# The first column tiles of a decoder step on x·g instead of the normalised x, with the factors applied at the end, and the sample states on column groups

## The chip, the cores and the metric

One core of a Trainium2 chip runs the whole program. The metric is the device time of one execution in microseconds (us). The engines are TensorE (PE: matmuls, and PEld: its weight loads), VectorE (DVE), ScalarE (ACT), GpSimd (POOL) and the queue of SyncE (SP), which here only issues DMAs.

## The reference, cut to what matters

One layer of a hybrid decoder for 1024 prompt tokens and 8 sample tokens (1032 columns in all), D = 1024, followed by a final norm:

```
h = rmsnorm(x, norm_g)               # x * rsqrt(mean(x^2) + eps) * g, per token
proj = h @ w_in                      # 7688 columns: q, k, v, beta, alpha, gate, u, v, ...
A) q, k, v = silu(causal_conv(...)); gated delta rule in chunks, one state per head
   sample tokens: S = a S + k (beta (v - a S^T k))^T ;  o = S^T q      (8 states x 4 heads)
B) chunked spatial gating:  u * (W_s layernorm(v) + b) * silu(gate)
C) cross-attention, 4 heads, into 256 memory tokens
merged = sum of sigmoid(gates) * (branch @ w_br);  y = rmsnorm(x + merged @ w_out)
```

Since a token's rsqrt factor is one number per token, (x·g·r) @ w equals ((x·g) @ w)·r.

## The kernel before, in words

Activations lie transposed: 128 channels on the partitions, 8 blocks k of channels, 1032 token columns. Every product is made of three passes of TensorE in a reduced format (fp32r): each operand is split in a rounded part `hi` and a rest `lo`, and `mm3` (L298) runs hi·hi, lo·hi and hi·lo, 24 matmuls for one group. `hTh` and `hTl` hold hi and lo of the normalised x for all columns. A column tile of `w_in` (128 output columns) is loaded (`w_load`), split by ACT and then DVE or POOL (`w_split`, L270), and multiplied with three groups of 344 token columns (`project`, L311). Two tiles are split ahead (`whi`, `wlo`, two buffers), four are loaded ahead (`raw`).

The order of all instructions is written out by hand. Long side chains are Python generators on a list `run`; `mm3` calls `tick()` after every sixth matmul, and each tick lets every generator emit its next piece, so the side work is strewn between the matmuls. Each engine runs its own instructions in the order in which they were emitted.

The opening (L361 to L550) cuts the columns in four parts (256, 256, 256, 264). For each part: `n_square` (L400) sums the squares of the untransposed x on ACT, `n_newton` (L404) takes the reciprocal root on DVE in 11 small instructions, `spread` (L317) makes a diagonal matrix of the factors on DVE and multiplies it with ones on PE, so that each partition has the token's factor, `scale` (L328, eight instructions) multiplies the transposed x by g and that factor in place, and `n_split` (L410) makes `hTh` and `hTl`. Then three column tiles ("k 0", "v 0", "bv 0") multiply that part, and ACT copies the results out (`evac`, L525; L534). Parts 1 to 3 are prepared by `norm_gen` while the matmuls of the part before run. Tile "q 0" follows as an ordinary `project` (L550), and then the narrow tile of 16 columns for beta and alpha (`wab2`, L580 to L588, 48 matmuls, "the ab stage" below), on which the gates and so the whole delta chain wait. The convolutions of k and v run on DVE (L500 to L507), that of q on POOL.

`sample_gen(h)` (L658) handles the 8 sample states of one head. Its matmuls (L687) take each state (128x128) as the weights and two columns (normalised k and q) as the moving operand: out comes S^T k and S^T q, with the channel on the partitions.

Of the kernel before, what the change touches and what calls it, by code (L numbers as in the profile page):

```python
# [151 lines left out]
def tile_mixer_step(ctx: ExitStack, tc: tile.TileContext, a):  # L152
# [175 lines left out]
    def scale(x, r, col, k):  # L328
        V.scalar_tensor_tensor(
            out=x[:, k], in0=x[:, k], scalar=colv[:, col + k:col + k + 1], in1=r, op0=ALU.mult, op1=ALU.mult  # L330
        )
# [68 lines left out]
    def n_square(i):  # L400
        x = xin[i][:rows[i]]
        S.activation(out=x, in_=x, func=AF.Square, accum_out=nss[:rows[i], i:i + 1])  # L402

    def n_newton(n):  # L404
        sl = slice(in_part[n][0], in_part[n][-1] + 1)
        x = nss[:, sl]
        V.tensor_scalar(out=x, in0=x, scalar1=1.0 / D, scalar2=EPS, op0=ALU.mult, op1=ALU.add)
        yield from rsqrt_ops(nrs[:, sl], x, f"n{n}")

    def n_split(n, b, eng=V):  # L410
        ks = slice(b * 4, b * 4 + 4)
        x, hi, lo = xT[n][:, ks], hTh[:, ks, part[n]], hTl[:, ks, part[n]]
        S.copy(out=hi, in_=x)
        eng.tensor_tensor(out=lo, in0=x, in1=f32(hi), op=ALU.subtract)

    def n_part(n):
        x = xT[n]
        r = spread(np_, nrs, [(i, rows[i]) for i in in_part[n]])
        yield
        for k in range(KT):  # L420
            scale(x, r, 0, k)
            if k % 2:
                yield
        n_split(n, 0)
        n_split(n, 1)
        done.add(("norm", n))

    n_square(0)
    n_square(1)
    for _ in n_newton(0):  # L430
        pass
    wsp = [w_split(0, eng=G), w_split(1, eng=G)]
    next(wsp[0])
    for _ in n_part(0):
        pass
    next(wsp[0], None)
    next(wsp[1])
    n_square(2)
    n_square(3)
    next(wsp[1], None)  # L440
    for _ in w_split(2, slow=False, eng=G, pool=np_):
        pass
    xt_load(2)
    x_load(5, 6)
    xt_load(3)
    x_load(7, 8)
    w_load(3)
    SP.dma_start(out=wab, in_=a["w_ab"])
    SP.dma_start(out=scT, in_=a["conv_old"])
    SP.dma_start(out=a["conv_kept"], in_=a["state_conv"][:, 1:3, :])  # L450

    def norm_gen():
        for n in range(1, 4):
            yield
            for i, _ in enumerate(n_newton(n)):
                if i % 4 == 3:
                    yield
            yield from n_part(n)
            if n < 3:
                for i in in_part[n + 1]:  # L460
                    n_square(i)
        split(wab2[:, :, 0:8], wab2[:, :, 8:16], wab)

    run.add(norm_gen())
# [48 lines left out]
    def qkv_tile(name, h):  # L513
        if name == "k":
            kq_t[h] = xp.tile([P, 2, NT], F32, tag="kq", name="kq")
            v_t[h] = xp.tile([P, NT], F32, tag="vt", name="vt")
# [5 lines left out]
        raw = xp.tile([P, 3 + NT], F32, tag="xraw", name="xraw", bufs=2)
        G.memset(raw[:, 0:3], 0.0)

        def evac(n, sl, o):  # L525
            S.copy(out=raw[:, 3 + sl.start:3 + sl.stop], in_=o)  # L526
# [10 lines left out]
    w3 = [splits.pop(i) for i in range(3)]
    for n in range(4):
        run.until(lambda: ("norm", n) in done)
        for i, (w, ev) in enumerate(zip(w3, evacs)):  # L540
            ev(NS - 1 if n == 3 else 0, *h_group(w, n, part[n]))
            if n == 3 and i == 0:
                w_load(4)
            if n == 3 and i == 1:
                for _ in w_split(3, slow=False):
                    pass
# [108 lines left out]

    ag_t = {}

    def sample_gen(h):  # L658
# [26 lines left out]
        r = tp()[:, 0:16].rearrange("p (b t) -> p t b", t=2)  # L685
        for b in range(NB):
            PE.matmul(r[:, :, b], lhsT=st[:, b], rhs=kqn[:, :, b], start=True, stop=True)  # L687
# [827 lines left out]
```

## Time and profile before

| what | value |
| --- | --- |
| median of 3 runs (lowest to highest) | 1172.46 us (1171.12 to 1173.76) |
| the profiled execution's own time | 1172.25 us |
| its span, first to last instruction | 1170.4 us |
| mean granted TensorE clock | 0.983 |
| PE busy | 1121.8 us (96%) |
| DVE busy | 614.2 us (52%) |
| ACT busy | 402.0 us (34%) |
| POOL busy | 231.3 us (20%) |

Busy times of an engine are sums of its instructions; what counts for the end is which engine is waited for in each stage. The profile gives, for every group of instructions, the idle time just before it and what ended it.

### The profile page before, as it was taken

The page shows a single profiled execution, that of the slowest core. Times are in us where ns is not written, and L with a number is a line of the kernel's source. Part 1 is how long each engine was busy: PE and PEld are TensorE (multiplying, and loading weights), DVE is VectorE, ACT ScalarE, POOL GpSimd, SP SyncE. Part 2 cuts the span into 40 slices and gives each one's busy share as a digit, 9 for nine tenths or more (in the row PEclk, how much of TensorE's full clock was granted, in tenths as well). Part 3 has the DMA queues.
Part 4 walks back from the last instruction along what each step waited for, and adds up shares of the span by engine and source line. Part 5 has one row for each costly group of instructions (what it writes and reads, how often), then busy time and mean ns, then how long its engine had stood idle before and what let it go on. Part 6 is the DMA issues. An engine that isn't in the chain of part 4 may idle for free.

```text
span 1170.4 us, 18943 instructions
## 1 busy us (share of the span) xinstructions
PE 1121.8 (96%) x7474; PEld 1072.8 (92%) x7474; DVE 614.2 (52%) x1534; ACT 402.0 (34%) x854; POOL 231.3 (20%) x394
## 2 busy tenths in 40 slices
PE   4699999999999999999899999899999999999997
PEld 4698999999999999999899999889999999998884
DVE  5553673477247635622376532646536256786554
ACT  3424323243333233323344313545445321232232
POOL 2015285035503550430033100101101000000000
PEclk8799999999999999999899999999999999999999
DMA  9022421232123312431544445344343356663221
GB/s 369 3 74 37 132 76 43 94 113 83 37 93 96 84 35 93 122 113 71 195 151 135 154 163 184 111 140 127 109 127 91 125 193 184 214 208 103 78 92 56
DMA packets 83034, 137.75 MB, mean 118 GB/s; under 512 B 21744, under 2 KB 51664, under 8 KB 82296
## 3 DMA queue, kind: packets, MB, share of 16 engines
q1 hardware_dynamic: 68960, 94.04, 24.6%
q10 hardware_dynamic: 13984, 42.49, 12.0%
q8 instruction: 59, 0.97, 0.3%
q14 instruction: 31, 0.25, 0.1%
HBM read 104.97 MB, written 31.64 MB: 117 GB/s over the span
## 4 chain that ended last, share of the span: by engine, by line
PE 86%; DVE 6%; ACT 3%; DMA 2%; issue 1%; SPq 0%; POOL 0%; ACTq 0%; DVEq 0%
PE pj L301 52%; PE dl L301 20%; PE dl L224 1%; PE tp L224 1%; PE dl L785 1%; ACT x L402 1%; PE dl L1133 1%; DVE wlo L279 1%; PE dl L919 1%; PE dl L895 1%; PE tp L1085 1%; PE dl L910 1%; PE dl L903 1%; PE tp L687 1%; DMA gcb<-gcd 1%
## 5 line engine op out<-in xcount | busy, mean ns | idle before, releaser
L301 PE MATMUL pj<-hTh,whi 128*128 128x344 f32 (+2 forms) x1464 | 284.6, 329 | 8.2 <-DVE ql L188 4.2
L301 PE MATMUL pj<-hTh,wlo 128*128 128x344 f32 (+2 forms) x1464 | 277.7, 324 | 0.0
L301 PE MATMUL pj<-hTl,whi 128*128 128x344 f32 (+2 forms) x1464 | 273.0, 325 | 0.0
L301 PEld LDWEIGHTS pj<-hTh,whi 128*128 128x128 f32 x1464 | 236.0, 193 | 11.3 <-DVE ql L188 4.5
L301 PEld LDWEIGHTS pj<-hTl,whi 128*128 128x128 f32 x1464 | 239.3, 193 | 0.9 <-issue 0.4
L301 PEld LDWEIGHTS pj<-hTh,wlo 128*128 128x128 f32 x1464 | 236.4, 191 | 1.5 <-issue 0.8
L279 DVE TENSOR_TENSOR wlo<-raw,whi 128x1024 fp32r<-128x1024 f32 (+1 forms) x89 | 97.5, 1095 | 45.4 <-ACT whi L276 45.2
L276 ACT CAST whi<-raw 128x1024 fp32r<-128x1024 f32 (+1 forms) x92 | 86.2, 937 | 75.7 <-PE dl L301 62.1
L839 POOL TENSOR_TENSOR itmp<-X,Lt 128x60 f32<-128x60 f32 (+24 forms) x124 | 53.0, 428 | 171.8 <-DMA Lt<-ld 162.5
L958 ACT COPY stg<-pj 128x344 f32<-128x344 f32 x72 | 32.1, 446 | 126.2 <-PE pj L301 122.5
L1190 POOL TENSOR_TENSOR kvt<-kvt,qb 128x1024 f32<-128x1024 f32 x8 | 19.3, 2433 | 215.0 <-DMA kvt<-cache_mem_v 215.0
L301 PE MATMUL dl<-yh,whi 128*128 128x344 f32 x288 | 57.4, 321 | 0.0
L301 PE MATMUL dl<-yl,whi 128*128 128x344 f32 x288 | 57.1, 320 | 0.0
L301 PE MATMUL dl<-yh,wlo 128*128 128x344 f32 x288 | 57.1, 320 | 0.0
L845 POOL TENSOR_TENSOR X<-X,itmp 128x60 f32<-128x60 f32 (+24 forms) x124 | 47.1, 380 | 9.7
L301 PEld LDWEIGHTS dl<-yl,whi 128*128 128x128 f32 x288 | 47.8, 188 | 0.0
L301 PEld LDWEIGHTS dl<-yh,whi 128*128 128x128 f32 x288 | 47.7, 188 | 0.0
L301 PEld LDWEIGHTS dl<-yh,wlo 128*128 128x128 f32 x288 | 47.5, 188 | 0.0
L526 ACT COPY xraw<-pj 128x344 f32<-128x344 f32 (+2 forms) x38 | 16.3, 430 | 89.0 <-PE pj L301 88.9
L907 DVE COPY y<-dl 128x128 f32<-128x128 f32 x32 | 9.3, 292 | 61.2 <-PE dl L905 39.9
L1373 DVE TENSOR_TENSOR stg<-dl,stg 128x344 f32<-128x344 f32 x48 | 24.7, 514 | 18.0 <-PE dl L301 18.0
L498 POOL TENSOR_TENSOR kq<-kq,cvt 128x512 f32<-128x512 f32 x24 | 33.5, 1394 | 1.9
(371 smaller groups left out, 1569.5 us busy)
## 6 DMA issues: line engine op xcount, KB each, us to landing
raw<-w_tiles ACTq DMA_DIRECT2D x65, 512.0 KB
gate<-stg SPq DMA_DIRECT2D x23, 516.0 KB
stg<-gate SPq DMA_DIRECT2D x23, 516.0 KB
raw<-w_br ACTq DMA_DIRECT2D x24, 256.0 KB
x<-x_prompt SPq DMA_DIRECT2D x8, 512.0 KB
kvt<-cache_mem_k SPq DMA_DIRECT2D x16, 256.0 KB
kvt<-cache_mem_v SPq DMA_DIRECT2D x16, 256.0 KB
wor<-w_out SPq DMA_DIRECT2D x8, 512.0 KB
```

The costliest lines, as they stand in the source:

```text
L224: PE.transpose(out, in_, ident[:p, :p])
L276: S.copy(out=hi, in_=raws[i])
L279: eng.tensor_tensor(out=lo, in0=raws[i], in1=f32(hi), op=ALU.subtract)
L301: PE.matmul(out, lhsT=w, rhs=r, start=(i == 0), stop=(i == len(ops) - 1))
L402: S.activation(out=x, in_=x, func=AF.Square, accum_out=nss[:rows[i], i:i + 1])
L498: G.tensor_tensor(out=d[:, cs], in0=d[:, cs], in1=o, op=ALU.add)
L526: S.copy(out=raw[:, 3 + sl.start:3 + sl.stop], in_=o)
L839: G.tensor_tensor(out=tm, in0=X[:, 0:m, j:j + 1].to_broadcast([P, m, n]), in1=Lt[:, j:j + 1, j + 1:32].to_broadcast([P, m, n]), op=ALU.mult,)
L845: G.tensor_tensor(out=X[:, 0:m, j + 1:32], in0=X[:, 0:m, j + 1:32], in1=tm, op=ALU.subtract)
L958: project("gate", i, lambda n, sl, o: S.copy(out=t[:, sl], in_=o))
L1190: G.tensor_tensor(out=kts[hb], in0=kts[hb], in1=qb[:, hb * 4:hb * 4 + 4].unsqueeze(2).to_broadcast([P, 4, 2, P]), op=ALU.mult,)
L1373: V.tensor_tensor(out=sg[:, sl], in0=o, in1=sg[:, sl], op=ALU.mult)
```

## The change

The first four tiles ("k 0", "v 0", "bv 0", "q 0") multiply x·g, without the factors. `hi_raw` (ACT, eight multiplications by g) and `lo_raw` (DVE, eight) make the two parts of x·g as soon as a part of x has arrived; squares, roots and spreads run behind, and the factors are kept in `rbc`. When a group is done, DVE multiplies the result by `rbc` while it copies it out (before: a plain copy on ACT). Behind that, x is normalised in place (`n_scale`) and `hTh`, `hTl` are written again (`n_again`) for all later tiles. "q 0" now also runs on the four parts. The first three weight tiles are split by DVE where POOL did it, the loads come in another order (transposed x ahead of x), tiles 4 and 5 are loaded from SP's queue, and 12 matmuls of ones run on PE at the start. In `sample_gen` the state becomes the moving operand and k, q (in a zero-padded block of 32 columns, `kqp`) the weights, at four column positions; the result, one row per token, is copied out by ACT and transposed twice by PE. An unused tile `pad` of 576 bytes per partition is added.

```diff
+    const.tile([P, 144], F32, name="pad")
...
-    x_load(0, 1)
     xt_load(0)
     SP.dma_start(out=colv, in_=a["cols"])
     w_load(0, SP)
-    x_load(2, 3)
+    x_load(0, 1)
     w_load(1, SP)
     xt_load(1)
     w_load(2, SP)
+    x_load(2, 3)
+    xt_load(2)
     x_load(4)
+    xt_load(3)
...
+    def n_spread(n):
+        t = tp()[:, :part[n].stop - part[n].start]
+        at = 0
+        for i in in_part[n]:
+            PE.matmul(t[:, at:at + rows[i]], lhsT=ones[:rows[i]], rhs=dgs[i], start=True, stop=True)
+            at += rows[i]
+        S.copy(out=rbc[:, part[n]], in_=t)
+
+    def hi_raw(n):
         for k in range(KT):
+            S.mul(out=hTh[:, k, part[n]], in_=xT[n][:, k], mul=colv[:, k:k + 1])
+
+    def lo_raw(n):
+        for k in range(KT):
+            V.scalar_tensor_tensor(
+                out=hTl[:, k, part[n]], in0=xT[n][:, k], scalar=colv[:, k:k + 1], in1=f32(hTh[:, k, part[n]]),
+                op0=ALU.mult, op1=ALU.subtract,
+            )
+
+    def n_scale(n):
+        for k in range(KT):
+            scale(xT[n], rbc[:, part[n]], 0, k)
+
+    def n_again(n):
+        for b in range(2):
+            ks = slice(b * 4, b * 4 + 4)
+            split(hTh[:, ks, part[n]], hTl[:, ks, part[n]], xT[n][:, ks])
+
+    t = tp()
+    for i in range(12):
+        PE.matmul(t[:, :P], lhsT=ident, rhs=ones, start=True, stop=True)
...
+    def raw_evac(n, tiles=(0, 1, 2)):      # -> V.tensor_tensor(out=..., in0=o, in1=rbc[:, sl], op=ALU.mult)
...
+    next(wsp[0])
+    hi_raw(0)
+    next(wsp[1])
+    lo_raw(0)
+    next(wsp[0], None)
+    next(wsp[1], None)
+    next(wsp[2])
+    next(wsp[2], None)
+    raw_group(0, 0, w3[0])
+    hi_raw(1)
+    w_load(3, SP)
+    n_square(0, 1)
+    raw_group(0, 1, w3[1])
+    lo_raw(1)
+    raw_group(0, 2, w3[2])
+    n_newton(0)
...
+    lo_raw(2)
+    n_square(2, 3)
+    raw_group(1, 1, w3[1])
+    n_spread(0)
+    raw_evac(0)
+    n_newton(1)
...
+    raw_group(2, 1, w3[1])
+    n_square(6, 7, 8)
+    n_scale(0)
+    raw_group(2, 2, w3[2])
+    n_spread(2)
+    raw_evac(2)
+    n_newton(3)
+    raw_group(3, 0, w3[0])
+    for _ in w_split(3, slow=False):
+        pass
+    n_spread(3)
+    raw_evac(3, (0,))
+    raw_group(3, 1, w3[1])
+    raw_evac(3, (1,))
+    n_scale(1)
+    raw_group(3, 2, w3[2])
+    raw_evac(3, (2,))
+    SP.dma_start(out=bv_d[0], in_=bv0)
+    w = splits.pop(3)
     for n in range(4):
+        raw_group(n, 0, w)
+        if n == 0:
+            run.until(lambda: ("k", 0) in done)
+            e_q = qkv_tile("q", 0)
+        e_q(NS - 1 if n == 3 else 0, part[n], held.pop((n, 0)), False)
+        n_again(n)
+        if n < 2:
+            n_scale(n + 2)
+        if n == 2:
+            for _ in w_split(4, slow=False):
+                pass
+            split(wab2[:, :, 0:8], wab2[:, :, 8:16], wab)
     nst.close()
-    project("q", 0, qkv_tile("q", 0))
...
         for b in range(NB):
-            PE.matmul(r[:, :, b], lhsT=st[:, b], rhs=kqn[:, :, b], start=True, stop=True)
+            rows = slice(32 * (b % 4), 32 * (b % 4) + 32)
+            PE.matmul(
+                t[rows, b // 4], lhsT=kqp[:, b], rhs=st[:, b], start=True, stop=True,
+                skip_group_check=True, tile_position=(0, 32 * (b % 4)),
+            )
+        rr = dp.tile([P, 2, P], F32, tag="p2", name="rr")
+        S.copy(out=rr, in_=t)
+        yield
+        t = tp()[:, :256].rearrange("p (g v) -> p g v", g=2)
+        for g_ in range(2):
+            transpose(t[:, g_], rr[:, g_])
```

More of the change, by code (lines that the diff above doesn't have):

```diff
@@ L393, in tile_mixer_step @@
     V.memset(nss, 1.0)
+    rbc = np_.tile([P, NT], F32, name="rbc")
     xst = ExitStack()
@@ L398, in tile_mixer_step, with n_square @@
     wab2 = xp.tile([P, KT, 16], F32R, name="wab2")
-    def n_square(i):
-        x = xin[i][:rows[i]]
-        S.activation(out=x, in_=x, func=AF.Square, accum_out=nss[:rows[i], i:i + 1])
+    def n_square(*tiles):
+        for i in tiles:
+            x = xin[i][:rows[i]]
+            S.activation(out=x, in_=x, func=AF.Square, accum_out=nss[:rows[i], i:i + 1])
     def n_newton(n):
@@ L407, in n_newton @@
         V.tensor_scalar(out=x, in0=x, scalar1=1.0 / D, scalar2=EPS, op0=ALU.mult, op1=ALU.add)
[L408 to L419, printed above, removed]
-        for k in range(KT):
[L421 to L464, printed above, removed]
+        for _ in rsqrt_ops(nrs[:, sl], x, f"n{n}"):
+            pass
@@ new lines, in n_newton @@
+        for i in in_part[n]:
+            dg = np_.tile([P, P], F32, tag="dg", name="dg", bufs=3)[:rows[i], :rows[i]]
+            V.tensor_scalar(
+                out=dg, in0=ident[:rows[i], :rows[i]], scalar1=nrs[:rows[i], i:i + 1], scalar2=None, op0=ALU.mult
+            )
+            dgs[i] = dg
+    def n_spread(n):
+        t = tp()[:, :part[n].stop - part[n].start]
+        at = 0
+        for i in in_part[n]:
+            PE.matmul(t[:, at:at + rows[i]], lhsT=ones[:rows[i]], rhs=dgs[i], start=True, stop=True)
+            at += rows[i]
+        S.copy(out=rbc[:, part[n]], in_=t)
@@ L523, in qkv_tile, with evac @@
         G.memset(raw[:, 0:3], 0.0)
-        def evac(n, sl, o):
-            S.copy(out=raw[:, 3 + sl.start:3 + sl.stop], in_=o)
+        def evac(n, sl, o, scaled=True):
+            if scaled:
+                S.copy(out=raw[:, 3 + sl.start:3 + sl.stop], in_=o)
+            else:
+                V.tensor_tensor(out=raw[:, 3 + sl.start:3 + sl.stop], in0=o, in1=rbc[:, sl], op=ALU.mult)
             if n == NS - 1:
@@ L533, in tile_mixer_step @@
     evacs = [
-        qkv_tile("k", 0), qkv_tile("v", 0), lambda n, sl, o: S.copy(out=bv0[:, sl], in_=o),
-    ]
-    w_pos[0] = 3
-    w3 = [splits.pop(i) for i in range(3)]
-    for n in range(4):
[L539 to L546, printed above, removed]
@@ L547, in tile_mixer_step, with raw_group @@
-    SP.dma_start(out=bv_d[0], in_=bv0)
-    run.until(lambda: not any(g for g in run.items if g[0].__name__ == "norm_gen"))
+        qkv_tile("k", 0), qkv_tile("v", 0),
+        lambda n, sl, o, scaled: V.tensor_tensor(out=bv0[:, sl], in0=o, in1=rbc[:, sl], op=ALU.mult),
+    ]
+    held = {}
+    def raw_group(n, i, w):
+        o = (pj if n % 2 == 0 and i < 2 else dl)()[:, :part[n].stop - part[n].start]
+        sl = part[n]
+        mm3(o, lambda k: w[0][:, k], lambda k: w[1][:, k], lambda k: hTh[:, k, sl], lambda k: hTl[:, k, sl], KT)
+        held[n, i] = o
@@ new lines, in raw_evac @@
+    def raw_evac(n, tiles=(0, 1, 2)):
+        for i in tiles:
+            evacs[i](NS - 1 if n == 3 else 0, part[n], held.pop((n, i)), False)
+    w_pos[0] = 4
+    wsp = [w_split(0), w_split(1), w_split(2, pool=np_)]
+    next(wsp[0])
[6 more added lines that the diff above has]
+    next(wsp[2], None)
+    w3 = [splits.pop(i) for i in range(3)]
+    raw_group(0, 0, w3[0])
+    hi_raw(1)
+    w_load(3, SP)
+    n_square(0, 1)
@@ new lines, in tile_mixer_step @@
+    raw_group(0, 1, w3[1])
+    lo_raw(1)
+    raw_group(0, 2, w3[2])
+    n_newton(0)
+    x_load(5, 6)
+    hi_raw(2)
+    raw_group(1, 0, w3[0])
+    lo_raw(2)
[4 more added lines that the diff above has]
+    n_newton(1)
+    raw_group(1, 2, w3[2])
+    hi_raw(3)
+    n_square(4, 5)
+    lo_raw(3)
+    raw_group(2, 0, w3[0])
+    n_spread(1)
+    raw_evac(1)
+    n_newton(2)
+    x_load(7, 8)
+    w_load(4, SP)
+    w_load(5, SP)
+    SP.dma_start(out=wab, in_=a["w_ab"])
@@ L656, in tile_mixer_step @@
     ag_t = {}
+    kqp = dp.tile([P, NB, 32], F32, name="kqp")
+    G.memset(kqp, 0.0)
     def sample_gen(h):
@@ L677, in sample_gen @@
         V.tensor_scalar(out=rn[:, 8:16], in0=rn[:, 8:16], scalar1=DKS, scalar2=None, op0=ALU.mult)
-        kqn = sm.tile([P, 2, NB], F32, tag="kqn", name="kqn")
+        kqn = kqp[:, :, 0:2].rearrange("p b t -> p t b")
         V.tensor_tensor(out=kqn, in0=kq, in1=rn.rearrange("p (t b) -> p t b", t=2), op=ALU.mult)
@@ L718, in sample_gen @@
             V.scalar_tensor_tensor(
-                out=st[:, b], in0=dbc[:, b], scalar=kqn[:, 0, b:b + 1], in1=st[:, b], op0=ALU.mult, op1=ALU.add
+                out=st[:, b], in0=dbc[:, b], scalar=kqp[:, b, 0:1], in1=st[:, b], op0=ALU.mult, op1=ALU.add
             )
```

18 lines of the change are left out of this document (15 added, 3 removed).

## The prediction

> **What bounds the kernel now.** I read the page's busy times first, then the busy times by stage, then who waited for whom in the opening, then the timeline of the opening and of the two places that the change touches.
>
> ```profile
> PE 1121.8 (96%) x7474; PEld 1072.8 (92%) x7474; DVE 614.2 (52%) x1534; ACT 402.0 (34%) x854; POOL 231.3 (20%) x394
> ```
> ```profile
> 0.00:85.35 85.35, 59.53 (x379) 58.04 (x379) 47.20 (x116) 31.26 (x50) 11.94 (x20) 0.88 0.41 153
> 85.35:1170.40 1085.05, 1062.26 (x7098) 1014.80 (x7095) 566.99 (x1418) 370.78 (x804) 219.39 (x374) 0.99 0.37 115
> ...
> 36.80:52.00 15.20, 10.07 (x57) 9.62 (x56) 8.09 (x24) 5.64 (x10) 0.00 (x0) 0.72 0.00 1
> 52.00:69.00 17.00, 17.00 (x129) 17.00 (x129) 6.06 (x12) 3.96 (x8) 0.00 (x0) 0.89 0.00 1
> ```
> ```profile
> PE dl L324 <- DVE dg L323: 22.7, 4, 9.5
> ```
> ```profile
> 13.52 1.22 PE L301 MATMUL pj<-hTh,whi 128*128 128x256 f32 x4 [2.83 <-ACT hTh L413]
> ...
> 85.35 0.31 PE L584 MATMUL pj<-hTh,wab 128*16 128x344 f32 x1
> ...
> 92.71 1.28 PEld L301 LDWEIGHTS pj<-hTh,whi 128*128 128x128 f32 x8
> ```
>
> Columns of the stages: stretch and length, busy time of PE, PEld, DVE, ACT, POOL, granted clock, DMA share, GB/s. PE is the bound: behind the first ab matmul (85.35 us, L584) it idles 1085.05 - 1062.26 = 22.8 us in 1085, ahead of it 25.8 us in 85. The waits say why: 22.7 us on the diagonal of the factors, that is on squares, roots and spread of each part. So what the opening saves reaches the end nearly whole, and I measure it at one point, the start of the ab stage, before at 85.35. Everything from there keeps its order, with the ab stage at 92.71 - 85.2 = 7.5 us.
>
> **The change part by part.** *PE's own work in the opening.*
>
> ```profile
> 28.78 1.01 PEld L301 LDWEIGHTS pj<-hTh,whi 128*128 128x128 f32 x8
> 29.73 1.03 PEld L301 LDWEIGHTS pj<-hTl,whi 128*128 128x128 f32 x8
> ...
> 36.80 1.83 PEld L301 LDWEIGHTS pj<-hTh,whi 128*128 128x128 f32 x8
> 38.51 1.82 PEld L301 LDWEIGHTS pj<-hTl,whi 128*128 128x128 f32 x8
> 40.22 1.82 PEld L301 LDWEIGHTS pj<-hTh,wlo 128*128 128x128 f32 x8
> 41.92 1.13 PEld L301 LDWEIGHTS pj<-hTh,whi 128*128 128x128 f32 x8
> ```
>
> Eight matmuls of 256 columns go in 29.73 - 28.78 = 0.95 us at full clock, a group of 24 in 2.86. Sixteen groups (four tiles on four parts; "q 0" costs the same columns as before) are 46 us and four spreads at most 0.8 each, 49 us in all. Started at 9 us, PE alone would have the ab stage at 58.
>
> *When the first operands are there.*
>
> ```profile
> GB/s 44 395 377 371 419 437 403 429 403 423 409 243 0 0 7 0 0 0 0 0 0 0 0 0 7 0 0 44 169 1 202 402 39 0 2 0 0 90 120 7
> ```
> ```profile
> 4.46 1.06 ACT L402 ACTIVATE x<-x 128x1024 f32<-128x1024 f32 x1 [2.17 <-DMA x<-x_prompt]
> 10.43 1.04 ACT L276 CAST whi<-raw 128x1024 fp32r<-128x1024 f32 x1 [3.65 <-DMA raw<-w_tiles]
> ```
>
> The DMAs run at about 0.4 MB per us (slices of 2.5 us) in the order of issue. Two landings are seen: 0.52 MB (first x) at 4.4, and 2.67 MB (x 0, x 1, transposed part 0, columns, w 0) at 10.4, a slope of 2.8 us per MB. After the change w 0 is at 1.62 MB: 7.5 us. ACT's queue has the split of w 0 ahead of `hi_raw`, so it starts there: 1.04 for the split and about 0.5 for the first multiplication, DVE's first `lo_raw` at 9.1 us. w 2 is at 4.77 MB, some 15.6, split on ACT by 16.7; DVE, done with `lo_raw` 0 (3.2 us) and two weight rests (1.18 each) at 14.7, waits there 2.0 us.
>
> *DVE's queue is the new bound.* It takes over the copying out (from ACT) and three weight rests (from POOL), and makes every operand twice, while the two convolutions stay ahead of `n_again`. Prices:
>
> ```profile
> 24.33 3.22 DVE L329 SCALAR_TENSOR_TENSOR xT<-xT,colv,dl 128x256 f32<-128x256 f32 x8 [1.12 <-PE dl L324]
> 30.45 2.36 DVE L414 TENSOR_TENSOR hTl<-xT,hTh 128x1024 fp32r<-128x1024 f32 x2 [2.90 <-ACT hTh L413]
> 33.48 0.17 DVE L407 TENSOR_SCALAR nss<-nss 128x2 f32<-128x2 f32 x1 [0.67 <-ACT x L402]
> 35.65 0.48 DVE L323 TENSOR_SCALAR dg<-ident,nrs 128x128 f32<-128x128 f32 x2
> ```
> ```profile
> 68.79 0.75 DVE L500 TENSOR_SCALAR kq<-xraw,colv 128x1024 f32<-128x1024 f32 x1 [8.05 <-ACT xraw L526]
> 69.59 1.28 DVE L505 SCALAR_TENSOR_TENSOR kq<-xraw,colv,kq 128x1024 f32<-128x1024 f32 x1
> 70.93 1.28 DVE L505 SCALAR_TENSOR_TENSOR kq<-xraw,colv,kq 128x1024 f32<-128x1024 f32 x1
> ```
> ```profile
> 928.96 0.52 DVE L1371 TENSOR_TENSOR merged<-dl,stg 128x344 f32<-128x344 f32 x1 [12.27 <-ACT stg L1404]
> 929.39 0.68 DVE L279 TENSOR_TENSOR wlo<-raw,whi 128x512 fp32r<-128x512 f32 x1
> ```
>
> - `lo_raw` and `n_scale`, four parts each: 8 x 3.22 = 25.8 us (same operation, shape and count as L329).
> - four roots with their diagonals: 33.48 to 35.65 + 0.48 = 2.65 each, one diagonal more for the last part: 10.8.
> - copying out, 12 groups and three of "q 0": an evacuation of 344 holds DVE 929.39 - 928.96 = 0.43, by width 0.34 for 256; 15 x 0.34 = 5.1.
> - weight rests of tiles 0 to 4: 2.36 / 2 = 1.18 each, 5.9.
> - `n_again` of parts 0 to 2: 3 x 2.36 = 7.1. The emitted order puts all three, the rest of tile 4 and that of `wab2` (0.2) ahead of the ab stage.
> - convolutions of k and v: 0.80 + 3 x (70.93 - 69.59 = 1.34) = 4.8 each, 9.6.
>
> Sum 64.5 us. From 9.1, with 2.0 of waiting for w 2 and about 1.4 of waiting for the spread of part 3 (PE and ACT need 0.8 and 0.4 once the diagonals are there), DVE reaches the rest of `wab2` at 77.0. The other inputs of that queue are early: evacuation of part 0 is due on DVE at about 27, PE ends the first group at 13.5 + 0.95 (rest of w 0, then eight matmuls) = 14.5, and four more and a spread at 14.5 + 4 x 2.86 + 0.6 = 26.5; each later part leaves more room. ACT's share (5 weight casts, 9 squares, 32 multiplications, 8 casts) is under 40 us. The multiplication by a column of factors is dearer than a copy:
>
> ```profile
> L1451 ACT ACTIVATE junk<-junk,frs x9: 718/725/727, 1078.4 to 1166.1; 128x512 f32<-128x512 f32 x8, 8x512 f32<-8x512 f32 x1
> ```
>
> 0.72 for 512 columns, so about 0.4 apart for 256, the pace of `lo_raw`; it hides behind DVE. SP's queue holds x 5 to x 8 until squares free their buffers (x 0's at about 20 us); behind them wait w 4, w 5, `wab`, all needed after 50 us: nothing. POOL's three rests are gone. So the ab stage starts at 77.0 instead of 85.35: 8.35 us gained. Bounds: 74.5 (w 2 no wait and `lo_raw` at 0.34 apart like the evacuation) to 81 (DVE durations instead of spacings, 0.08 on each of 40-odd pieces).
>
> *PE goes cold meanwhile.* Its last "q 0" group ends at about 63 (58 plus waits for `lo_raw` 0 and the spread of part 3), then it idles 14 us. In the rows above, PE back at 35.99 after 4.1 us of idling loads eight weights in 1.71 instead of 0.95 until 41.9: 5.9 us at little over half rate (the stage shows 0.72). On the ab stage that costs 5.5 x 0.45 = 2.5 us; bounds 0 (no loss) to 3.
>
> The Trainium skill, page "TensorE: Matmul & The Clock Gate" (Part 1), says the array runs at half clock by default, is released after about 3.4 us of sustained work and falls back after an idle window of that length; the idle 4.1 us with 5.9 slow us behind them agree in kind and are longer than the page's window. By the page alone the loss would be about 1.7 us (an estimate), and the sum 0.8 us better.
>
> *The sample states.*
>
> ```profile
> 144.59 1.90 PEld L687 LDWEIGHTS tp<-kqn,st 128*128 128x128 f32 x16
> 146.41 0.30 PEld L301 LDWEIGHTS pj<-hTh,whi 128*128 128x128 f32 x2
> ```
> ```profile
> 779.10 0.38 PEld L1221 LDWEIGHTS tp<-kvt,pTs 128*32 128x32 f32 x16 [0.21 <-issue]
> 779.68 0.93 PEld L301 LDWEIGHTS pj<-hTh,wlo 128*128 128x128 f32 x6 [0.20 <-issue]
> ```
> ```profile
> 140.34 0.51 PEld L224 LDWEIGHTS dl<-ident,kq 128*128 128x128 f32 x4
> 140.82 0.30 PEld L301 LDWEIGHTS pj<-hTh,whi 128*128 128x128 f32 x2
> ```
>
> Per head PE loses 146.41 - 144.59 = 1.82 us to L687. The same shape as the new one stands at L1221: 779.68 - 779.10 and an idle 0.21 ahead, 0.79. Two transposes add half of 140.82 - 140.34 = 0.48: 0.24. Gain 0.8 per head, 3.2 for four. The transposes wait for ACT's copy, with a tick of six matmuls (0.95 us) ahead; bounds 0 (ACT queue full, PE waits 0.8) to 4.
>
> *The rest.* The tile `pad` and the zeroing of `kqp` (POOL, early): 0, covered by the wait of all `dp` work for the ab stage. The 12 matmuls of ones lie before 9 us where PE has nothing: 0.
>
> Sum: 8.35 - 2.5 + 3.2 = 9.0 us. Profiled time 1172.25, 0.2 under the median: 1163.2 us. The forecast's own bounds are 4.35 - 3 + 0 = 1 and 10.85 + 4 = 15 us of gain, all ends together; most of it between 5 and 13, 1159 to 1167.
>
> **The rivals.**
> 1. *PE-bound opening.* If DVE's pieces come out shorter, the ab stage follows "q 0" at 63 with a warm array: 22.3 + 3.2, 1147 us. For: DVE was only 47.2 busy in 85 before. Against: the prices are of the same operations and shapes; DVE's sum would have to shrink by 14 of 64.5.
> 2. *The gain is given back.* POOL's convolution of q (it starts with the last "q 0" evacuation, now just ahead of the ab stage as before) or the gates' DVE chain ends later relative to PE, and PE waits there. Price: up to the whole 9; 1170 to 1174. For: PE waited at L633 for that chain, as the waits from 93 us on show. Against: 1.6 us was all, and the order there is the same.
>
> ```profile
> PE tp L633 <- DVE gp L629: 1.6, 1, 1.6
> ```
>
> 3. *Slower: the array stays at half clock.* The first groups are fed one 256-column piece per 0.4 us, and PE idles between. Decisive from about six raw groups at half rate: 9 + 6 x 5.5 = 42, six more at 2.86, and DVE still has its last 36 us behind the spreads of part 2 (due then at 52 instead of 41): ab stage at 88. If nine groups are slow, 61 + 36 = 97, the gain becomes -11.7 - 2.5 + 3.2: 1183 us. For: at 36.80 to 52 the clock was 0.72 with PE two thirds busy. Against: from 52 on PE was back at full rate within 6 us, and 12 matmuls warm it.
>
> **How the numbers follow.** About 0.2% (2.3 us) is what a measurement can tell from no change. Forecast (DVE-bound, faster by 4 to 15) 0.60; rival 1, including ends between 1147 and 1157, 0.14; rival 2, 0.14; rival 3, 0.12. Faster 0.75 (forecast and rival 1), same 0.13, slower 0.12. The range from 1149 to 1172 leaves out rival 3 and the far ends of the two others; the forecast's own is 1158 to 1168.
>
> **What would show it.** First ab matmul (L584's successor) at 77, with DVE as releaser and 10 to 15 us of PE idle before it: right. A first raw matmul at about 9 (before: 13.52) and DVE over 85% busy from 9 to 77 confirm the sum; a first ab matmul near 63 means rival 1, a granted clock under 0.75 over the raw groups rival 3. For the states: 16 records of the new matmul within 0.8 us. The forecast is wrong if DVE waits elsewhere in its queue, above all for the spread of a part, or if PE's idle time behind 92 us exceeds the 22.8 of before by more than 2.

## Result and profile after

The changed kernel takes 1163.22 us in the median of five runs (1160.35 to 1165.11), against 1171.12 us of the kernel before in the same comparison (1168.99 to 1173.76, five runs). The ratio is 0.9927, with a 95% interval of 0.9905 to 0.9949: faster by 0.7%, some 8 us. The profiled execution took 1163.22 us as well, its span is 1161.5 us (before 1170.4), so the two profiles differ by 8.9 us. The forecast was 1163.2 us.

The page of the changed kernel, busy times:

```profile
PE 1119.0 (96%) x7530; PEld 1070.1 (92%) x7530; DVE 637.7 (55%) x1585; ACT 412.2 (35%) x879; POOL 230.8 (20%) x392
```

DVE has 23.5 us more work, ACT 10 us more, PE 2.8 less: the gain isn't in the sums. The table of stages of the changed kernel (stretch and length, busy time of PE, PEld, DVE, ACT, POOL, granted clock, DMA share, GB/s), cut at the first raw matmul, the first ab weight load, the end of the ab stage, the gates' gp matmul, the first transposes of k and q, and the first block of sample states:

```profile
9.26:77.83 68.57, 54.07 (x402) 52.66 (x402) 63.06 (x161) 37.55 (x68) 5.19 (x8) 0.85 0.37 142
77.83:86.79 8.96, 8.96 (x47) 5.07 (x48) 6.86 (x8) 0.87 (x2) 8.43 (x6) 0.80 0.02 2
86.79:101.00 14.21, 13.68 (x81) 13.15 (x78) 9.00 (x23) 5.53 (x9) 9.62 (x9) 0.88 0.21 74
101.00:109.48 8.48, 8.45 (x54) 8.24 (x55) 1.60 (x3) 6.88 (x10) 1.10 (x8) 1.00 0.65 31
109.48:141.77 32.29, 30.16 (x183) 29.19 (x182) 18.22 (x60) 11.18 (x44) 4.98 (x14) 0.95 0.42 129
```

The same four stages of the kernel before, from its ab stage on:

```profile
85.19:92.71 7.52, 7.52 (x50) 4.56 (x49) 1.18 (x2) 1.31 (x3) 6.48 (x6) 1.00 0.01 1
92.71:106.48 13.77, 12.12 (x81) 11.59 (x78) 8.65 (x23) 5.48 (x9) 9.23 (x8) 1.00 0.12 39
106.48:116.42 9.94, 9.94 (x54) 9.52 (x55) 1.61 (x3) 6.98 (x10) 1.10 (x8) 0.83 0.44 43
116.42:144.59 28.17, 28.17 (x182) 27.64 (x182) 18.03 (x60) 11.18 (x44) 5.15 (x15) 1.00 0.46 141
```

Read side by side, the opening ends 7.36 us earlier. Then the ab stage takes 1.44 more, the stage to the gates 0.44 more, the next 1.46 less and the last 4.12 more: by the first sample block only 2.82 us are left. From there, by the weight loads of both traces: first to fourth block of sample states 342.22 before and 339.27 after (2.95 gained), on to the first output matmul 576.33 and 575.09 (1.24 gained, with the fourth block in it), the output stage from its first to its last weight load 98.59 and 96.12 (2.47 gained), and what follows 0.5 lost. Sum 2.82 + 2.95 + 1.24 + 2.47 - 0.53 = 8.95.

Who waited for whom, PE in the changed kernel (us in total, times, longest):

```profile
PE pj L652 <- DVE wab L188: 12.1, 1, 12.1
...
PE tp L426 <- DVE dg L417: 2.4, 1, 2.4
PE pj L302 <- ACT stg L1066: 2.1, 1, 2.1
...
PE pj L302 <- ACT stg L1045: 1.1, 1, 1.1
...
PE tp L701 <- DVE gp L697: 0.6, 1, 0.6
```

The 22.7 us on the diagonals of before are 2.4; in their place stands one wait of 12.1 us on the two parts of `wab`, DVE's last piece ahead of the ab stage. And there are two waits on evacuations by ACT that before doesn't have: one of 2.1 us that ends at 114.7 us, in the last stage of the table, and one of 1.1 us far behind it, between 570 and 575 us.

### The profile page after: what moved, and what is told of

It is laid out like the page before. It is cut to its first block, busy times and chain, and to the rows that moved or that the text cites. A ratio compares the mean times of both kernels' runs of the same rounds, so it can differ in the third digit from the quotient of the medians.

```text
span 1161.5 us, 19130 instructions
## 1 busy us (share of the span) xinstructions
PE 1119.0 (96%) x7530; PEld 1070.1 (92%) x7530; DVE 637.7 (55%) x1585; ACT 412.2 (35%) x879; POOL 230.8 (20%) x392
## 4 chain that ended last, share of the span: by engine, by line
PE 84%; DVE 8%; DMA 4%; ACT 2%; issue 1%; SPq 0%; ACTq 0%; POOL 0%; DVEq 0%
PE pj L302 49%; PE dl L302 21%; PE tp L225 1%; PE dl L225 1%; PE dl L872 1%; DVE xT L330 1%; PE dl L1220 1%; DMA x<-mem_prompt 1%; PE dl L1006 1%; PE tp L1172 1%; PE dl L982 1%; PE dl L990 1%; PE dl L997 1%; DMA sbg<-g 1%; PE dl L1005 1%
## 5 line engine op out<-in xcount | busy, mean ns | idle before, releaser
L302 PE MATMUL pj<-hTh,whi 128*128 128x344 f32 (+1 forms) x1392 | 273.8, 331 | 9.6 <-DVE ql L188 3.4
L302 PE MATMUL pj<-hTh,wlo 128*128 128x344 f32 (+1 forms) x1392 | 267.1, 326 | 0.0
L302 PE MATMUL pj<-hTl,whi 128*128 128x344 f32 (+1 forms) x1392 | 260.1, 325 | 0.0
L302 PEld LDWEIGHTS pj<-hTh,whi 128*128 128x128 f32 x1392 | 225.3, 191 | 13.9 <-DVE ql L188 3.6
L302 PEld LDWEIGHTS pj<-hTh,wlo 128*128 128x128 f32 x1392 | 225.7, 190 | 1.9 <-issue 1.2
L302 PEld LDWEIGHTS pj<-hTl,whi 128*128 128x128 f32 x1392 | 226.7, 191 | 0.8 <-issue 0.2
L280 DVE TENSOR_TENSOR wlo<-raw,whi 128x1024 fp32r<-128x1024 f32 (+1 forms) x92 | 100.5, 1094 | 44.4 <-ACT whi L277 44.2
L926 POOL TENSOR_TENSOR itmp<-X,Lt 128x60 f32<-128x60 f32 (+24 forms) x124 | 48.7, 393 | 174.0 <-DMA Lt<-ld 164.7
L1045 ACT COPY stg<-pj 128x344 f32<-128x344 f32 x72 | 32.1, 446 | 121.4 <-PE pj L302 121.3
L932 POOL TENSOR_TENSOR X<-X,itmp 128x60 f32<-128x60 f32 (+24 forms) x124 | 54.3, 438 | 9.7
L516 ACT COPY xraw<-pj 128x344 f32<-128x344 f32 x27 | 12.0, 444 | 59.9 <-PE pj L302 59.9
```

What stands on the lines that cost most here:

```text
L280: eng.tensor_tensor(out=lo, in0=raws[i], in1=f32(hi), op=ALU.subtract)
L302: PE.matmul(out, lhsT=w, rhs=r, start=(i == 0), stop=(i == len(ops) - 1))
L926: G.tensor_tensor(out=tm, in0=X[:, 0:m, j:j + 1].to_broadcast([P, m, n]), in1=Lt[:, j:j + 1, j + 1:32].to_broadcast([P, m, n]), op=ALU.mult,)
L932: G.tensor_tensor(out=X[:, 0:m, j + 1:32], in0=X[:, 0:m, j + 1:32], in1=tm, op=ALU.subtract)
L1045: project("gate", i, lambda n, sl, o: S.copy(out=t[:, sl], in_=o))
```

## Experiments

All are edits of the changed kernel, except the one with `pad` alone. Times are medians; the ratio is to the kernel before, run beside each of them on the same chip, so two runs are compared by their ratios. The changed kernel stands at 0.9927.

| run | what | us (runs) | ratio [95%] |
| --- | --- | --- | --- |
| e1_more_dve | 6.4 us more on DVE in the opening | 1166.67 (5) | 0.9949 [0.9935, 0.9963] |
| e2_old_states | sample states as before | 1168.02 (5) | 0.9957 [0.9944, 0.9971] |
| e3_no_pad | without `pad` | 1164.38 (5) | 0.9920 [0.9905, 0.9934] |
| e4_pad_only | kernel before with `pad` | 1170.76 (11) | 0.9986 [0.9971, 1.0001] |
| e5_early_wab | `wab` split early | 1159.72 (4) | 0.9880 [0.9862, 0.9899] |
| e6_warm_fill | 40 fill matmuls in the idle time | 1161.17 (6) | 0.9899 [0.9881, 0.9918] |
| e7_late_as | the delta chain and the gate of the states 4 ticks later | 1167.50 (6) | 0.9955 [0.9937, 0.9973] |
| e8_no_warm | no warm-up matmuls | 1164.18 (6) | 0.9926 [0.9908, 0.9944] |
| e9_apart_as | that gate alone later | 1158.46 (5) | 0.9900 [0.9884, 0.9915] |
| e10_q0_dve | `wab` early, convolution of "q 0" on DVE | 1156.76 (6) | 0.9889 [0.9868, 0.9909] |
| e11_warm_fill58 | 58 fill matmuls | 1165.30 (6) | 0.9960 [0.9945, 0.9975] |
| e12_combined | e5, e9 and e10 together | 1154.15 (5) | 0.9853 [0.9826, 0.9879] |

### Is DVE the bound of the opening?

The theory is that DVE's queue sets the start of the ab stage; the rival, that another input (PE's groups, a landing) does. The rests of two parts are computed twice:

```diff
     lo_raw(2)
+    lo_raw(2)
...
     lo_raw(3)
+    lo_raw(3)
```

> The changed kernel with lo_raw of parts 2 and 3 issued twice: 16 more DVE instructions (3.25 us each eight, as in the trace of the changed kernel), the same results. Theory (DVE's queue sets the start of the ab stage): first ab matmul at 77.8 + 6.4 = 84.2 us and the whole 6.4 us longer, about 1169.6. Rival (PE or the DMAs set it, DVE has slack): first ab matmul stays within 2 us of 77.8 and the time within 2 us of 1163.

Its stretch from the first raw matmul to the ab stage:

```profile
8.60:82.40 73.80, 55.48 (x403) 53.61 (x404) 69.39 (x177) 37.63 (x68) 5.19 (x8) 0.85 0.35 136
```

DVE's busy time rose by 69.39 - 63.06 = 6.3 us, the stretch by 73.75 - 68.57 = 5.2 (82.35 is the first ab weight load): five sixths of what was added. DVE bounds the opening; its idle time fell by 1.1 us, from 5.5 to 4.4, and took up the rest. The ab stage starts 4.5 us later, at 82.35 (84.2 was expected), since this execution's first raw matmul came 0.66 us earlier: short of the theory, and clear of the rival's 2 us. The ratio rose by 0.0022, some 2.6 us, less than the 5.2 and less than expected; the two intervals overlap.

If DVE's whole queue is the bound, what the ab stage needs of it can be put first. e5 splits `wab` ahead of all `n_again`, and weight tile 4 behind the last of them:

```diff
     w = splits.pop(3)
+    split(wab2[:, :, 0:8], wab2[:, :, 8:16], wab)
...
-        if n == 2:
+        if n == 3:
             for _ in w_split(4, slow=False):
                 pass
-            split(wab2[:, :, 0:8], wab2[:, :, 8:16], wab)
```

> The changed kernel with the split of wab2 ahead of the q groups and the split of weight tile 4 behind n_again of part 3. The first ab group needs only parts 0 and 1, which DVE has done at 69.8 us. Theory (order in DVE's queue sets the start): first ab matmul at about 70, the second third at 76.3, the third at 78.8; the ab stage ends at 82 to 83.5 instead of 86.9, and the time is 3 to 4.5 us less, about 1159. Rival (what is gained is waited for at the gates or tile 4's rest): ab stage earlier, the time within 1 us of 1163.

The first ab matmuls start at 65.1 instead of 77.8 (70 was expected) and then wait, part by part, for the later rests of x. The ab stage ends at 81.2 instead of 86.8, 5.6 earlier. But the gates' gp matmul comes at 99.2 instead of 101.0, only 1.8 earlier:

```profile
PE tp L701 <- DVE gp L697: 3.1, 1, 3.1
```

So the change's order wastes time ahead of the ab stage, and most of what is saved there meets the next limit, the gates' chain on DVE (3.1 us, in the changed kernel 0.6). The whole is faster than the changed kernel (the intervals don't touch), with the forecast of 1159 met. The trace is of the slowest of e5's four executions, 1163.20 us, and shows no gain at its end: the granted clock is at half for 6.83 us from 98.43 on, at the gp wait (see "The clock").

### What holds the gates' chain?

DVE in e5, beside POOL's convolution of "q 0" (which ends at 96.2 there):

```profile
87.08 1.07 DVE L670 TENSOR_TENSOR abt<-abt,al_bc 128x36 f32<-128x36 f32 x1
88.19 0.94 DVE L672 TENSOR_SCALAR e<-abt 128x36 f32<-128x36 f32 x1
...
94.94 1.33 DVE L684 TENSOR_TENSOR s<-s 128x36 f32<-128x36 f32 x1
96.30 0.20 DVE L685 TENSOR_SCALAR e<-s 128x36 f32<-128x36 f32 x1
```

Most of the 36-column instructions take about 1 us each until POOL is done, then 0.20. e10 takes POOL's share away, with `wab` early as in e5:

```diff
-        if key[0] == "q":
+        if key[0] == "q" and key[1]:
...
-            if key[0] != "q":
+            if key[0] != "q" or not key[1]:
```

> e5 (early split of wab2, late split of tile 4) with the convolution of q of head 0 on DVE, as for k and v, instead of POOL. In e5 the ab stage ended 5.6 us earlier but the gates' first matmul (gp) only 1.8 us, with DVE's gate instructions 1 us each while POOL ran that convolution. Theory (POOL's tensor instructions hold DVE's up): gate instructions 0.2 us each, gp at about 93 to 94 instead of 99.2, 3 to 6 us less than e5, about 1155. Rival (the 4.8 us more on DVE cost as much, or the DMA round trip behind the gates decides): gp not earlier than 97, the time within 1 us of e5's 1159.7.

```profile
88.45 0.20 DVE L670 TENSOR_TENSOR abt<-abt,al_bc 128x36 f32<-128x36 f32 x1
...
91.45 0.20 DVE L684 TENSOR_TENSOR s<-s 128x36 f32<-128x36 f32 x1
...
94.27 0.18 DVE L697 COPY gp<-g 128x32 f32<-128x32 f32 x1
```

The same instructions without POOL take 0.20. The chain from L666 to gp shrinks from 12.3 us in e5 to 6.3, and gp is there at 94.4. That is shown: beside POOL's convolution these small DVE instructions take about five times as long. It did not all reach the end: PE comes to gp at 97.4 with no wait, instead of the 93 to 94 expected. Its own matmuls hold it up, since the granted clock is at half from 85.24 to 92.07 us in this trace; those 6.83 us at half rate cost 3.4, about the difference. The evacuation wait at L1066 comes out larger, too (2.2 us, 0.4 in e5). By the place of gp and by its ratio e10 did what its rival said, though DVE's instructions did what the theory said. The step of 1.8 us from e5's 99.2 is shown in the trace; between the two whole times (0.9880 and 0.9889) there is no difference that can be measured. The Trainium skill, page "SBUF — State Buffer" (Who interferes with whom), says that VectorE and GpSimd share a port pair under an exclusive lock, which a VectorE instruction needs for two inputs in SBUF or in a two-port mode, and that the loser stands still for the other's whole instruction. DVE's 0.94 to 1.33 us beside POOL's instructions of about 1.03 and 1.29 us agree with that.

### The wait on ACT

ACT in the changed kernel and in the kernel before, at the exponential of the sample states' gate:

```profile
114.06 0.26 ACT L721 ACTIVATE as__875<-sbb 128x32 f32<-128x32 f32 x1 [5.10 <-DMA sbb<-sbg]
114.23 0.43 ACT L1066 COPY stg<-pj 128x344 f32<-128x344 f32 x1
```
```profile
118.62 0.26 ACT L653 ACTIVATE as__768<-sbb 128x32 f32<-128x32 f32 x1 [3.83 <-DMA sbb<-sbg]
```

ACT waits for a small DMA (`sbb`, the factors broadcast by way of memory), and an evacuation that PE needs stands behind (L1066; the 1.1 us at L1045 come over 450 us later and are not this wait). Before, the wait is 3.83 us and costs PE nothing; after, it is 5.10 and PE waits 2.1. From the gp matmul to this instruction it was 12.14 us before and 13.06 after, while PE's own work from gp to the transposes shrank from 9.94 to 8.48. The work is the same: in the kernel before, PE ran this stage at a clock of 0.83, after, at 1.00. So what had covered ACT's wait was in part a spell of half rate. Two ways to move the instruction were tried. e7 lets the generator of the gates wait four ticks longer:

```diff
         done.add("gates")
-        yield 5
+        yield 9
```

> The changed kernel with the exponential of the sample decays (ACT, waits 5.1 us for the DMA of sbb in the changed kernel's trace, with evacuations queued behind it) emitted four ticks later. Theory (that ACT wait holds up PE by about 2 us behind the gates, more than before the change): PE no longer waits there, 1.5 to 2.5 us less, about 1161. Rival (the wait moves to the next instruction that needs the DMA, or the slow clock there stays): within 1 us of 1163.

The evacuation waits are gone from its list, and yet its ratio is higher than the changed kernel's (0.9955 against 0.9927; the intervals overlap a little). In their place, in the first head's chain:

```profile
PE dl L951 <- DVE TA L943: 3.9, 2, 2.4
PE dl L952 <- DVE T L944: 1.8, 3, 0.9
```

In the changed kernel these are 0.5 and 0.2 us. The expectation was wrong, and so was its rival: `delta_all` runs `gates_gen` to its end before it begins the first head, so the whole chain came four ticks later (first transposes at 111.95, 3.8 us behind the 108.11 of e9, which has the same opening), and PE met it. e9 delays nothing but the two instructions and the flag of the sample states:

```diff
         done.add("gates")
+        run.add(late_gen(sbb))
         yield 5
+
+    def late_gen(sbb):
+        yield 10
         V.tensor_copy(out=bs, in_=sbb[:, :, 0].rearrange("p b h -> p h b"))
```

> The changed kernel with the two sample-decay instructions (copy of beta, exponential of g, which wait for the DMA of sbb) in a generator of their own, emitted ten ticks behind the gates instead of five, while the delta chain starts after five as before. e7, which moved them by delaying the whole chain, showed PE free of the ACT wait but the chain four ticks later. Theory (both are true: ACT's wait holds PE by 2 to 3 us, and the chain's start counts): the PE waits on evacuations at L1045 and L1066 (3.2 us) go, the chain keeps its place, 2 to 3 us less than the changed kernel, about 1160.5. Rival (any later start of the sample states costs as much): within 1 us of 1163 or more.

Its stretch from the transposes to the first sample block:

```profile
108.11:137.34 29.23, 28.62 (x183) 27.56 (x182) 18.25 (x60) 12.34 (x44) 4.72 (x12) 1.00 0.47 142
```

29.23 us against 32.29 in the changed kernel: 3.1 us. Half of it is idle time of PE (0.61 instead of 2.13 us: the wait of 2.1 is gone, one of 0.6 on LA stands in its place). The other half is the clock, 1.00 instead of 0.95, which leads to the next part. The ratio is 0.9900 against 0.9927 (the intervals just overlap). The profiled execution is 4.9 us shorter, but 1.4 of that is there already at the gp matmul (99.62 instead of 101.00), ahead of the edit: a spell of half rate at 91.57 us in the changed kernel's trace is not in e9's.

### The clock

The forecast had PE cold at the ab stage for 2.5 us. The ab weight loads of the changed kernel:

```profile
78.10 0.14 PEld L652 LDWEIGHTS pj<-hTh,wab 128*16 128x16 f32 x1
78.39 0.14 PEld L653 LDWEIGHTS pj<-hTl,wab 128*16 128x16 f32 x1
...
81.25 0.14 PEld L653 LDWEIGHTS pj<-hTl,wab 128*16 128x16 f32 x1
81.45 0.09 PEld L652 LDWEIGHTS pj<-hTh,wab 128*16 128x16 f32 x1
81.61 0.09 PEld L653 LDWEIGHTS pj<-hTl,wab 128*16 128x16 f32 x1
```

Up to 81.25 they stand 0.29 us apart, then 0.16: the stage takes 8.96 instead of 7.52, 1.44 lost. e6 and e11 fill the idle time with matmuls that nothing uses (40 or 58 of them):

```diff
+    t = tp()
+    for _ in range(40):
+        PE.matmul(t[:, :P], lhsT=ident, rhs=ones, start=True, stop=True)
     for n in range(NS):
```

> The changed kernel with 40 matmuls of ones (128x128, results unused) on PE between the last q group and the ab stage, where it idles 12 us. Theory (PE is cold at the ab stage since it idled): all ab matmuls 0.157 us apart, the stage 7.5 instead of 9.1 us, 1.6 us less in all, about 1161.6. Rival (the ab matmuls are slow for their operands' sake or the saved time is waited for at the gates): stage 9 us, or the time unchanged.

> As e6 but with 58 filling matmuls (0.227 us each in e6's trace: 13.2 us from 64.1, to 77.3), so that PE idles less than 1 us ahead of the ab stage; in e6 it idled 3.41 us and its ab matmuls were again 0.287 apart for 6 us. Theory: all ab matmuls 0.157 apart, the stage 7.5 us, its end at 84.3 to 85 instead of 86.6; the time 1 to 2 us less than the changed kernel, unless the gates' chain takes it. Rival (the ab matmuls are slow of themselves when they start): stage 9 us or more.

The ab stage in e6, then in e11:

```profile
76.60:86.45 9.85, 9.85 (x47) 5.41 (x48) 6.85 (x8) 0.87 (x2) 9.25 (x7) 0.72 0.01 1
```
```profile
77.15:84.63 7.48, 7.48 (x51) 4.58 (x50) 6.26 (x7) 0.87 (x2) 7.32 (x5) 1.00 0.01 1
178.60:188.80 10.20, 9.99 (x109) 9.12 (x110) 4.62 (x7) 1.55 (x4) 8.77 (x7) 0.51 0.01 2
```

40 fills end too early: 3.41 us of idling remain, and the stage is as slow as 9.85 us. So e6 doesn't test the cold price, and its time (0.9899) isn't told apart from the changed kernel's (0.9927): the intervals overlap. 58 fills reach up to the ab stage, which takes 7.48 us at clock 1.00: the cold price is confirmed. But nothing is won. The gp matmul of e11 comes at 99.34, that of e8 (no fills, and no matmuls at the start) at 99.54; and at 178.6 PE runs 10.2 us at half rate, some 5 us lost, behind new waits of 2.1 and 0.7 us in the first head's chain. The whole is 0.9960, above the changed kernel's and e8's 0.9927 and 0.9926 (the interval touches that of the changed kernel and is clear of e8's). Why the chain is late there was not settled.

What the spells of half rate have in common shows when the trace is cut 3.4 us before each, here in the kernel before (107.3), in the changed kernel (115.8) and in e11 (178.6):

```profile
103.90:107.30 3.40, 1.75 (x12) 1.34 (x11) 2.12 (x11) 0.00 (x0) 0.00 (x0) 0.95 0.00 0
107.30:110.70 3.40, 3.40 (x14) 3.10 (x13) 0.38 (x2) 2.94 (x6) 0.00 (x0) 0.54 0.03 5
```
```profile
112.40:115.80 3.40, 1.27 (x8) 1.09 (x7) 0.26 (x2) 1.74 (x12) 0.00 (x0) 0.95 0.40 160
115.80:119.20 3.40, 3.40 (x15) 3.40 (x14) 3.06 (x9) 1.27 (x9) 0.00 (x0) 0.55 0.00 0
```
```profile
175.20:178.60 3.40, 0.76 (x6) 0.36 (x4) 0.71 (x2) 0.06 (x1) 3.24 (x4) 0.95 0.28 43
```

Each time PE was busy 0.76 to 1.75 us out of 3.40 (the waits of 1.6, 2.1 and 2.1 + 0.7 us), and the next stretch runs at half rate: 3.4 us of it cost 1.7. So a wait of 2 us can cost almost 4. It need not: in e6 the same evacuation holds PE up for 1.8 us, PE is busy 1.90 of 3.42 us (109.41 to 112.83), and the clock stays at 1.00; in e12 PE is busy 1.68 of 3.41 (78.85 to 82.26), and full rate follows too. Such a spell is half of the 3.1 us that e9 wins, the 1.7 that the kernel before lost behind its gp wait, and most of what e11 lost.

Another spell in the changed kernel, at 91.57, has no idle time ahead of it, but 18 matmuls of 8 columns for the gates (L664, 88.95 to 91.12); in e9 the same matmuls are followed by no spell. The traces show what differs. Within one trace all changes of the granted clock lie whole multiples of 3.41 us apart: in the changed kernel it falls to half at 9.65, 47.20, 67.68, 91.57, 115.46, 559.20 and 726.45 us, for 3.41, 6.83 or 13.65 us. On this raster the 18 matmuls lie within one stretch in the changed kernel (88.16 to 91.57), in e1, e2, e3 and e11, and in e5 but for 0.14 us; half rate follows in all six. In the kernel before, e4, e6, e7, e8 and e9 a line of the raster cuts them at least 0.27 us from an end (in e9 at 89.27, the matmuls from 88.69 to 90.86), and it follows in none. In e10 and e12 PE also waits there. No run varied the raster by itself.

e8 takes out the 12 matmuls of ones at the start:

> The changed kernel without the 12 matmuls of ones at the start. Theory (DVE sets the opening, PE has room): first groups slow until about 15 to 18 us; DVE waits at the spread of part 0 by 0 to 3 us more; the time 0 to 2 us longer. Rival (the clock of the first groups decides): PE late by 5 us or more, the time 4 us or more longer.

With 0.9926 against 0.9927 they are worth nothing that can be measured. They didn't keep PE at full rate either: in the changed kernel the clock is at half from 9.65 to 16.48 us, and in e8 the weight loads reach the pace of 0.95 us for eight by 14.6.

### Sample states, and the tile `pad`

e2 puts the old `sample_gen` back (state as weights, two columns moving) and leaves the rest:

```diff
-            PE.matmul(
-                t[rows, b // 4], lhsT=kqp[:, b], rhs=st[:, b], start=True, stop=True,
-                skip_group_check=True, tile_position=(0, 32 * (b % 4)),
-            )
+            PE.matmul(r[:, :, b], lhsT=st[:, b], rhs=kqn[:, :, b], start=True, stop=True)
```

> The changed kernel with the sample states as before (state as weights, two columns moving). Theory (the states on column groups give about 0.85 us per head to PE): 3.4 us longer than the changed kernel, about 1166.6, so the opening alone is worth 5 to 6. Rival (PE hides or regains that time, all the gain is the opening's): within 1 us of 1163.

Weight loads of the first block in the changed kernel:

```profile
141.77 0.38 PEld L759 LDWEIGHTS tp<-st,kqp 128*32 128x32 f32 x16 [0.21 <-issue]
142.34 0.30 PEld L302 LDWEIGHTS pj<-hTh,whi 128*128 128x128 f32 x2 [0.20 <-issue]
...
143.24 0.30 PEld L225 LDWEIGHTS tp<-ident,rr 128*128 128x128 f32 x2
143.51 0.61 PEld L302 LDWEIGHTS pj<-hTl,whi 128*128 128x128 f32 x4
```

The block takes 0.57 and 0.21 us of idling ahead, 0.78, the two transposes 0.27, against 1.82 before. Matched weight load by weight load, the offset between the traces of before and after jumps by 0.82, 1.16, 0.79 and 0.71 us at the four blocks, 3.48 in all (the second with a wait of 0.38 us on DVE behind the block that is gone after); in e2 about 4.0 are lost again there. e2's ratio is 0.9957, about the 3.4 us more that were expected, with an interval that overlaps the changed kernel's. Its trace shows a second loss elsewhere: its output stage takes 98.47 us, that of the changed kernel 96.12. The difference is in the pace of 512-column matmuls. Eight weight loads each, kernel before and then after:

```profile
1072.40 1.82 PEld L301 LDWEIGHTS dl<-woh,ml 128*128 128x128 f32 x8
1074.27 1.82 PEld L301 LDWEIGHTS dl<-woh,mh 128*128 128x128 f32 x8
```
```profile
1068.75 1.77 PEld L302 LDWEIGHTS dl<-wol,mh 128*128 128x128 f32 x8
1070.57 1.77 PEld L302 LDWEIGHTS dl<-woh,ml 128*128 128x128 f32 x8
```

1.87 and 1.82 us for eight; 384 matmuls make 2.4 us of it. Nothing in the change touches this stage, but two things move the tiles in memory: `pad`, and the block `kqp` in place of the small tile `kqn`. Both were undone by themselves:

```diff
-    const.tile([P, 144], F32, name="pad")
```

> The changed kernel without the unused tile of 576 bytes per partition. Theory (the output stage's matmuls of 512 columns go every 0.227 instead of 0.233 us since all tiles behind that one lie elsewhere): spacing back to 0.233, about 2.5 us longer, 1165.7. Rival (the pace has another cause, or none): spacing 0.227 and 1163 within 1 us.

> The kernel before with only that unused tile added. If placement sets the pace of the output stage: 0.227 us per matmul there and about 2.5 us less than before, ratio 0.998. Otherwise: no difference beyond 0.2%.

Output stage from the first to the last weight load: kernel before 98.59, with `pad` alone (e4) 98.48, new states without `pad` (e3) 97.73, both (changed kernel and the nine kernels made from it that keep both) 96.11 to 96.12. `pad` does nothing without the new states and 1.6 us with them, less than the 2.5 expected. Its worth in the whole time isn't shown: e3's 0.9920 is no different from 0.9927, and e4's 0.9986 is within 0.2% of no change. That the place of the tiles in memory sets the pace is argued from this; which tile and why was not tried.

### All together

> The changed kernel with the three edits that shortened it put together: wab's copies issued early (e5), the q convolution of tile 0 on VectorE (e10), and sbb computed apart from the DMA that two evacuations waited behind (e9). e10 alone stood at 1156.8 us, and its trace still had PE waits of 2.2 and 1.7 us on the evacuations L1066 and L1045, the ones that e9 took away. If the gains add, 1156.8 less 3 to 4 us: about 1153, a ratio to before of about 0.985, and both waits under 0.5 us each. Rival: once the evacuations are free, PE waits as long on the next link of the delta chain (TA, or the gates' gp), as in e7; then the time stays within 1 us of e10's, 1156 to 1158, with a new PE wait of 2 us or more on DVE in the stretch after the gates.

e12 takes 1154.15 us, ratio 0.9853, the lowest of all: 0.7% below the changed kernel and 1.5% below the kernel before; its interval overlaps those of e5 and e10. Its two longest waits of PE between the ab stage and the first sample block:

```profile
PE tp L664 <- DVE sel L660: 2.8, 1, 2.8
PE dl L876 <- DVE LA L877: 1.5, 1, 1.5
```

The evacuation waits are gone, as expected (0.2 us is left at the later one), and the time is a us above the 1153 of the sum. DVE, which now has the convolution too, makes PE wait 2.8 us at the gates' first matmuls (1.4 in e10) and 1.5 us in the chain: the new wait that the rival named is there, but not its time.

## Why the prediction came out

The time came out as forecast and the opening is the mechanism forecast, but the total is better than its terms: the first two were off by 1 us each, and two places put at nothing held a loss of 3.1 and a gain of 2.5. They cancelled; that the total was met to the tenth is luck. Signs are gains:

| step | predicted | profiled |
| --- | --- | --- |
| start of the ab stage | +8.35 (at 77.0) | +7.4 (at 77.83) |
| cold PE at the ab stage | -2.5 | -1.4 |
| gates to the first sample block | 0 | -3.1 |
| four blocks of sample states | +3.2 | +3.5 |
| output stage | 0 | +2.5 |
| everything else | 0 | +0.2 (sum of +0.7 and -0.5) |
| sum | +9.05 | +9.0 |

*The opening* went as described. The rows on DVE that answer to the prices:

```profile
9.24 3.28 DVE L436 SCALAR_TENSOR_TENSOR hTl<-xT,colv,hTh 128x256 fp32r<-128x256 f32 x8 [8.30 <-ACT hTh L432]
...
16.45 1.23 DVE L280 TENSOR_TENSOR wlo<-raw,whi 128x1024 fp32r<-128x1024 f32 x1 [1.66 <-ACT whi L277]
...
21.74 0.17 DVE L412 TENSOR_SCALAR nss<-nss 128x2 f32<-128x2 f32 x1 [0.90 <-ACT x L407]
...
28.59 0.76 DVE L518 TENSOR_TENSOR xraw<-pj,rbc 128x256 f32<-128x256 f32 x2 [0.96 <-ACT rbc L428]
...
69.81 4.09 DVE L330 SCALAR_TENSOR_TENSOR xT<-xT,colv,rbc 128x264 f32<-128x264 f32 x8
```

DVE starts at 9.24 (predicted 9.1), `lo_raw` takes 3.28 (3.22), the wait for w 2 is 1.66 (2.0), and DVE is busy 63.06 of 68.57 us, 92% (over 85% was forecast). Three items that the forecast lacked made it late: 0.90 on the squares, 0.96 on the copied spread, and `n_scale` of the last part at 4.09 instead of 3.2, beside a POOL instruction (1.08 us at 70.1). Most of it came back, and 0.8 us is left: the 1.4 us put down for the spread of part 3 was not on DVE (there PE waited for DVE, 2.4), and w 2 came sooner. By the forecast's own slope of 2.8 us per MB w 2 would have landed at 16.3 us, not at the 15.6 it wrote; ACT began to split it at 15.37, so the slip did no harm.

*The cold array* was oversized by 1 us, because the price was taken from a spell of 5.9 us in the trace of before, while the spell here ended after 3.4 us. The Trainium skill's 3.4 us (page "TensorE: Matmul & The Clock Gate", Part 1), which gave 1.7, was nearer in this run; in e6 the stage ran at 9.85, 2.3 us above 7.52, near the 2.5. Both lengths occur, and the trace of before had both. The page's rule that an idle window of about 3.4 us is needed is not what the runs show: 1.6 us of waiting within 3.4 were enough (103.90 to 107.30 above).

*The gates* are the step that failed: "everything from there keeps its order", with nothing lost behind 92 us. The order was kept, but a wait of 3.83 us on ACT that was covered before lost its cover when PE came sooner and ran the stage ahead of it at full clock: PE waited 2.1 us, and that drew a spell of half rate with it. Rival 2 had the right place, and the named link (the gates' chain beside POOL's convolution) was there too, though it only bites once the ab stage is earlier than in this change: 0.6 us here, 3.1 in e5. The sign of failure that was set, PE's idle time behind 92 us more than 2 us above 22.8, didn't show it: 23.9 us. It did not look at the clock.

*The sample states* were right in mechanism and nearly in size (block 0.78 for 0.79, transposes 0.27 for 0.24). *Rival 1* is excluded by PE's idle 12.1 us ahead of the ab stage, *rival 3* by a granted clock of 0.91 over the groups of the first four tiles (9.26 to 65.5; the 0.85 of the table takes in PE's idle time behind them). What was held against rival 3, that 12 matmuls warm the array, was wrong all the same: half rate lasted to 16.48 us. *The output stage* was put at nothing, `pad` with it; 2.5 us came from there, which no row of before could have told.
